# Convolution stage: two output weights loaded after the last way back, one tap ordered behind a low part, one tap moved ahead

## The chip, the cores and the metric

The kernel runs on one core of one Trainium2 chip. The time is that of one execution on the device in microseconds; a kernel's time is the median of several runs. The engines are named as in the profile: PE (TensorE, matrix products), DVE (VectorE), ACT (ScalarE), POOL (GpSimd), SP (SyncE, which issues most of the loads), and PEld for PE's weight loads.

## What is computed

Two layers of a trunk, each a token mixer followed by a SwiGLU network: first a convolution module, then sparse attention. SEQ is 512, D_MODEL 1024, float32 throughout. The change lies in the convolution module, the first 157 us:

```python
CONV_WIDTH = 31

def conformer_conv_module(h, w_in, b_in, w_dw, b_dw, ln_g, ln_b, w_out):
    a, g = jnp.split(h @ w_in + b_in, 2, axis=-1)
    u = a * jax.nn.sigmoid(g)
    u = lax.conv_general_dilated(
        u, w_dw[:, None, :].astype(u.dtype), window_strides=(1,),
        padding=[(CONV_WIDTH - 1, 0)], dimension_numbers=('NWC', 'WIO', 'NWC'),
        feature_group_count=D_MODEL) + b_dw
    uf = u.astype(jnp.float32)
    mu = jnp.mean(uf, axis=-1, keepdims=True)
    var = jnp.mean(jnp.square(uf - mu), axis=-1, keepdims=True)
    uf = (uf - mu) * lax.rsqrt(var + LN_EPS) * ln_g.astype(jnp.float32) + ln_b.astype(jnp.float32)
    u = jax.nn.silu(uf).astype(h.dtype)
    return u @ w_out
```

`h` is the normalised input. A projection gives `a` and `g`, the gated product `u` is convolved along time with 31 taps for each channel, normalised over the channels, and projected out. Then follow the network, the attention and a second network.

## The kernel before

**Chunks.** Channels lie on the 128 partitions, so the 1024 channels are 8 chunks of 128, and time (512) lies along the free axis.

**Weights.** Weights come in units of 128 x 1024 floats that are numbered in the order of use: 4 to 17 for chunks 1 to 7 of the input projection (two for each chunk, `a` and `g`), 18 to 21 for the first half of the output projection, 22 to 25 for its second half. A product in full precision is made of three: SP loads a raw tile `wr` (L216, three buffers), ACT copies its high part to `wh` (L226, two buffers), DVE subtracts to get the low part `wl` (L235, two buffers), and PE multiplies high by high (L286), high by low (L287) and low by high (L288). A weight's high part is requested one weight ahead of its use, its low part in the middle of the tile before.

**Who convolves.** After each projection the gate (`glu`, L488 to L498) makes the chunk's `u`, with DVE (L489, L492, L498) and ACT (L490). Chunk 0 is convolved on DVE, one `scalar_tensor_tensor` for each tap (L515). Chunks 2 and 3 share theirs: DVE does 22 and 18 taps, the other 9 and 13 are a product on ACT (L533, tile `tap`, four buffers) and an addition on POOL (L539), and L541 joins the halves. Chunk 1 is ACT and POOL alone. These taps of ACT and POOL stand in a list from which `some_taps` takes a few at a time: `TAPS_AT[i]` says how many ahead of and behind the `g` projection of chunk i. DVE's taps are issued with a high priority, so the scheduler fills them in between its other work.

**PE's chunks.** Chunks 4 to 7 are convolved on PE (L586, tile `cpe`). For that `u` is first rearranged by way of DRAM, eight phases of 64 time steps over 16 channels at a time: SP stores it (L560) and loads it back as `uf` (L561). The band matrices `bd` come by POOL's queue (L462), three buffers for four chunks. DVE evacuates the product (L590), ACT squares it (L592), SP stores the evacuated tile (L591) and loads it back in the order of channels (L568): the *way back*. Chunk 7 is done in four parts (`SPLIT`), and so are its evacuations and stores.

**Normalisation.** PE sums the convolved chunks and their squares over the channels (L637, `lnst`, for chunks 0 to 3; L649, `lng`, for chunks 4 to 7). ACT copies `lnst` (L656, `rows`), PE transposes it (L659, `lnrt`), DVE reduces both (L663 to `st`, L668 to `red`), and a chain of small steps on DVE, ACT and PE spreads mean and scale. Then for each chunk DVE subtracts and multiplies, ACT applies the activation twice (L798, `a` and `lny`), and DVE makes the low part (L784). The output projection begins with chunk 0 (L377, L378, L383) and goes on as the chunks are ready; each two chunks use one weight of 18 to 21.

**Order.** The order on each engine is fixed at build time by a scheduler. `after(a, b)` adds the condition that a stands behind b in that order, and no wait of its own. An engine runs its instructions in order, so whatever stands behind a waiting one waits too. Behind the last projection, L762 to L764 ask for weights 18 to 20 behind the load of chunk 7's `uf`, L766 keeps every later load of SP behind chunk 7's way back, and L768 and L769 ask for weight 18's parts.

Of the kernel before, what the change touches and what calls it, by code (L numbers as in the profile page):

```python
# [15 lines left out]
ALU = mybir.AluOpType  # L16
# [40 lines left out]
PE_CONV = (4, 5, 6, 7)  # L57
SHARED = {2: 9, 3: 13}
SHIFTED = (3,)
TAPS_AT = {2: (4, 3), 3: (4, 3), 4: (4, 3), 5: (4, 3), 6: (4, 3), 7: (4, 3)}  # L60
LN_ORDER = (0, 1, 2, 3)
BAND_BUFS = 3
SPLIT = {7: 2}
# [64 lines left out]
def trunk(ctx: ExitStack, tc: tile.TileContext, A, out):  # L128
    nc = tc.nc
# [8 lines left out]
    def nm(s):  # L138
        cnt[0] += 1
        return f"{s}_{cnt[0]}"  # L140
# [51 lines left out]
    raws, raw_dma, split, los = {}, {}, {}, set()  # L192
    pin = {}

    def after(a, b):

        if b is not None:
            tc.add_manual_dep(a.ins, b.ins.name, mybir.DependencyInfo(
                mybir.DependencyClass.NoSync, mybir.DependencyReason.DATA), reason="order")
        return a  # L200

    state = {"next": 0, "end": 18}
    hold = [False]

    def held(ins):
        return tc.keep_in_program_order(ins) if hold[0] else ins

    def parted(ins):
        return ins if hold[0] == "pe" else held(ins)

    def w_dma(i):
        if i in raws or i >= len(units):
            return
        ap, cols = units[i]
        t = wp.tile([P, 1024], F32, tag="wr", name=f"wr{i}")
        raw_dma[i] = parted(after(nc.sync.dma_start(t[:, :cols], ap), state.get("behind")))  # L216
        raws[i] = t
# [11 lines left out]
    def w_lo(i=None):  # L229
        i = state["next"] if i is None else i  # L230
        if i in los or i not in split:
            return
        cols = units[i][1]
        hi, lo = split[i]
        parted(after(nc.vector.tensor_tensor(lo[:, :cols], raws[i][:, :cols], hi[:, :cols], ALU.subtract), pin.get(ALU)))  # L235
        los.add(i)

    def next_w(ahead=True):

        i = state["next"]  # L240
        w_hi(i)
        w_lo(i)
        state["next"] += 1
        if ahead and i + 1 < state["end"]:
            w_hi(i + 1)
        for k in range(i, min(i + 4, state["end"])):
            w_dma(k)
        return split[i]
# [25 lines left out]
    def v(col, n=1):  # L274
        return vec[:, col:col + n]
# [74 lines left out]
    def norm_b(r, pool, tag):  # L350

        ps2 = pool.tile([P, T], F32, tag=tag, name=nm("rbc"))
        for t in range(4):
            held(nc.tensor.matmul(ps2[:, t * P:(t + 1) * P], r[:, t:t + 1].to_broadcast([P, P]), ident,
                                  start=True, stop=True))
        R = tp.tile([P, T], F32, tag="Rb", name=nm("Rb"), bufs=1)
        nc.scalar.activation(R, ps2, AF.Copy)
        return R
# [35 lines left out]
    def proj_tile(pool, tag, xh=None, xl=None, mid=None, fixed=False):  # L394
        xh, xl = xh or hh, xl or hl
        ps = pool.tile([P, T], F32, tag=tag, name=nm("pp"))
        wh, wl = next_w()
        for k in range(NK):
            c = slice(k * P, (k + 1) * P)
            if fixed:  # L400
                kept = tc.keep_in_program_order
                kept(nc.tensor.matmul(ps, wh[:, c], xh[k], start=k == 0, stop=False))
                kept(nc.tensor.matmul(ps, wh[:, c], xl[k], start=False, stop=False))
                kept(nc.tensor.matmul(ps, wl[:, c], xh[k], start=False, stop=k == NK - 1))
            else:
                mm3(ps, wh[:, c], wl[:, c], xh[k], xl[k], k == 0, k == NK - 1)
            if k == 3:
                w_lo()
                if mid:
                    mid()  # L410
        return ps
# [27 lines left out]
    def conv_module():  # L439
        acc = new_acc()  # L440
        with ExitStack() as cx:
# [25 lines left out]
            for k in range(NK):  # L467
                split_x(k, V_NM0)
                if k % 2 == 0:
                    wh, wl = next_w()  # L470
# [11 lines left out]
            last = {}  # L482
# [4 lines left out]
            def glu(i, pA, pG):  # L487
                gr = ct.tile([P, T], F32, tag="A", bufs=3, name=f"gr{i}")  # L488
                y = nc.vector.tensor_tensor(gr, pG, R, ALU.mult)  # L489
                last["glu_act"] = nc.scalar.activation(gr, gr, AF.Sigmoid, bias=v(V_BG + i))  # L490
                ar = pA
                after(nc.vector.tensor_tensor(ar, pA, R, ALU.mult), y)  # L492
                if i in PE_CONV:
                    dst = u[i][:, 32:].rearrange("p (r t) -> p t r", r=8)
                    ar, gr = (z.rearrange("p (t r) -> p t r", r=8) for z in (ar, gr))
                else:
                    dst = u[i][:, 32:]
                last["glu"] = nc.vector.scalar_tensor_tensor(dst, ar, v(V_BA + i), gr, ALU.add, ALU.mult)  # L498

            def wtap(i, j):  # L500
                return wdw[:, i * TAPS + j:i * TAPS + j + 1]

            def conv_dve(i):
                c = pc.tile([P, T], F32, tag="pc", name=f"cv{i}")
                if i in SHIFTED:
                    b = ct.tile([P, T], F32, tag="ptap", name=nm("bs"), bufs=1)
                    nc.scalar.activation(b, sh["s"], AF.Identity, scale=-1.0, bias=v(V_BDW + i))
                    z = nc.vector.scalar_tensor_tensor(c, u[i][:, 2:2 + T], wtap(i, 0), b, ALU.mult, ALU.add)
                else:
                    z = nc.vector.tensor_scalar(c, u[i][:, 2:2 + T], wtap(i, 0), v(V_BDW + i), ALU.mult, ALU.add)  # L510
                after(z, last.get("dve"))
                n = TAPS - SHARED.get(i, 0)
                for j in range(1, n):
                    dst = vch[i] if j == TAPS - 1 else c
                    last["dve"] = nc.vector.scalar_tensor_tensor(dst, u[i][:, 2 + j:2 + j + T], wtap(i, j), c,  # L515
                                                                 ALU.mult, ALU.add)
                if i in SHARED:
                    parts[i] = c
                vt[i] = vch[i]

            taps, parts = [], {}

            def conv_pool(i, j0=0):
                c = cp.tile([P, T], F32, tag="pacc", bufs=2, name=nm("pv"))
# [21 lines left out]
            def some_taps(n):  # L546
                for _ in range(n):
                    if taps:
                        taps.pop(0)()
# [152 lines left out]
            def after_glu(i):  # L702
                if i in PE_CONV:
                    ups[i] = conv_pe_load(i)
                else:
                    if i in POOL_CONV:
                        conv_pool(i)
                        return
                    if i not in SHIFTED:
                        conv_on_v(i)  # L710
# [7 lines left out]
            def at(i):  # L718
                for z in CONV_AT.get(i, ()):
                    if z == "s":  # L720
                        ln_shift(LN_ORDER[0])
                    elif z == "p":
                        some_taps(len(taps))
                    elif z[0] == "d":
                        conv_on_v(int(z[1:]))
                    elif z == "t":
                        ln_tok()
                    elif z == "w":
                        sh["w"] = pc.tile([P, T], F32, tag="pc", name="warm")
                    elif z[0] == "n":  # L730
                        sh[z] = ln_stat(LN_ORDER[int(z[1:])])
                    elif z[0] == "m":
                        ln_sum(int(z[1:]), sh["n" + z[1:]])
                    elif z[0] == "g":
                        ph_sum(int(z[1:]))
                    else:
                        c = int(z[1:])
                        conv_pe(PE_CONV.index(c), c, ups[c])

            for i in range(1, NK):  # L740
                pA = proj_tile(pm, "pm", mid=norm_1 if i == 1 else None, fixed=i == 1)

                def gated():
                    glu(i - 1, *pend)
                    after_glu(i - 1)

                def norm_2():
                    nonlocal R
                    R = norm_b(last["r"], pa, "pa")
                    gated()  # L750

                if i > 1:
                    gated()
                some_taps(TAPS_AT.get(i, (0, 0))[0])
                pG = proj_tile(pm, "pm", mid=norm_2 if i == 1 else None, fixed=i == 1)
                some_taps(TAPS_AT.get(i, (0, 0))[1])
                pend = (pA, pG)
                at(i)
            glu(NK - 1, *pend)
            after_glu(NK - 1)  # L760
            state["end"] = len(units)
            for k in range(18, 21):  # L762
                w_dma(k)
                after(raw_dma[k], last["load"])  # L764
            at(8)
            state["behind"] = last["back"]  # L766
            pin.update(last["evac"])
# [1462 lines left out]
```

## Time and profile before

| | us |
|---|---|
| time, median of 3 runs | 1188.76 |
| lowest and highest run | 1188.07 to 1189.54 |
| the profiled execution's own time | 1188.95 |
| its span (first to last instruction in the trace) | 1187.2 |
| PE busy | 1166.4 |
| DVE busy | 945.9 |
| ACT busy | 640.8 |
| POOL busy | 303.7 |

The profiled execution's time is 1.75 us longer than the span, which lies outside of the recorded instructions, and 0.19 longer than the median. The granted clock was 0.999 of full speed over the span, so no throttling has to be reckoned with.

In the rows below, a line of the totals gives busy time, share of the span and the count of instructions. A row of the waits says which engine and tile waited, for whom, and the sum, the count and the longest wait. A row of the timeline gives the start in us from the span's start, the stretch that the group occupies, engine, line, operation, tile written and tiles read, shapes, count, and in brackets the idle time before it and what ended it; "SPq" and "POOL DMA" are issues of transfers. A row of the windows gives, for a stretch of 2 us, its length and then for each of PE, PEld, DVE, ACT and POOL the busy time and the count, then the granted clock, the share of the DMA engines and the GB/s.

### The profile page before, as it was taken

The numbers are of one execution on the slowest core, as the hardware profiler recorded it, in microseconds if no ns is written. First come the engines' busy times: TensorE is split into PE (matmuls) and PEld (weight loads), VectorE is DVE, ScalarE is ACT, GpSimd is POOL, SyncE is SP. The second block draws the span as 40 slices with busy tenths as digits, with TensorE's granted clock in tenths as the row PEclk, the third lists the DMA queues.
The fourth block names the chain that finished last, engine by engine and source line by source line (L and its number), as shares of the span: only waits on it lengthen the run. The fifth ranks groups of instructions, "written<-read, shape, count | busy, mean of one in ns | idle before, by whom it ended". The sixth has DMA issues, their size and how long they took to land.

```text
span 1187.2 us, 20756 instructions
## 1 busy us (share of the span) xinstructions
PE 1166.4 (98%) x7653; PEld 993.2 (84%) x7653; DVE 945.9 (80%) x1872; ACT 640.8 (54%) x1199; POOL 303.7 (26%) x398
## 2 busy tenths in 40 slices
PE   9999999999999999999999999999999999999998
PEld 6778688799999889997778777668878999998998
DVE  6999797889999787972667778865597999986876
ACT  5665664455555445553444678773355555554543
POOL 2699001011111101210233566760000111110120
PEclk9999999999999999999999999999999999999999
DMA  8634627367777768663455101025324787775892
GB/s 301 264 109 132 181 91 228 107 170 188 186 189 186 182 188 196 125 188 97 128 153 157 46 19 36 10 71 143 107 94 137 185 186 186 184 192 143 230 187 98
DMA packets 80310, 178.13 MB, mean 150 GB/s; under 512 B 29264, under 2 KB 30928, under 8 KB 79184
## 3 DMA queue, kind: packets, MB, share of 16 engines
q1 hardware_dynamic: 56896, 105.78, 28.2%
q0 software_dynamic: 23312, 71.02, 26.8%
q8 instruction: 60, 0.98, 0.3%
q14 instruction: 42, 0.34, 0.1%
HBM read 161.93 MB, written 4.75 MB: 140 GB/s over the span
## 4 chain that ended last, share of the span: by engine, by line
PE 88%; DVE 6%; issue 2%; ACT 2%; DMA 1%; SPq 0%; POOL 0%; DVEq 0%; ACTq 0%; POOLq 0%
PE st L983 40%; PE pp L286 9%; PE pp L288 9%; PE pp L287 9%; PE O L1952 3%; PE T L1926 3%; PE S L1895 2%; PE cpe L586 2%; PE st L287 2%; PE st L286 2%; PE st L288 2%; PE S L1896 1%; DVE wl L235 1%; PE pv L1769 1%; PE pp L377 1%
## 5 line engine op out<-in xcount | busy, mean ns | idle before, releaser
L983 PE MATMUL st<-bo,sh 128*128 128x256 f32 (+1 forms) x952 | 245.6, 333 | 0.4 <-DVE t L1019 0.4
L226 ACT ACTIVATE wh<-wr 128x1024 fp32r<-128x1024 f32 (+3 forms) x146 | 151.2, 1035 | 166.7 <-issue 57.1
L235 DVE TENSOR_TENSOR wl<-wr,wh 128x1024 fp32r<-128x1024 f32 (+3 forms) x146 | 178.5, 1222 | 44.9 <-ACT wh L226 44.8
L983 PE MATMUL st<-bo,sl 128*128 128x256 f32 x680 | 191.7, 282 | 0.0
L983 PEld LDWEIGHTS st<-bo,sh 128*128 128x128 f32 x952 | 160.9, 189 | 20.2 <-DVE t L1019 1.2
L286 PE MATMUL pp<-hh,wh 128*128 128x512 f32 x400 | 158.6, 399 | 2.3 <-ACT wh L226 1.9
L288 PE MATMUL pp<-hh,wl 128*128 128x512 f32 x400 | 157.7, 397 | 2.2 <-DVE wl L235 2.2
L287 PE MATMUL pp<-hl,wh 128*128 128x512 f32 x400 | 157.5, 395 | 0.1
L983 PEld LDWEIGHTS st<-bo,sl 128*128 128x128 f32 x680 | 129.0, 190 | 0.0
L969 DVE TENSOR_TENSOR sl<-S,sh 128x512 fp32r<-128x512 f32 x136 | 90.6, 688 | 22.5 <-ACT sh L968 22.4
L983 PE MATMUL st<-bo,wh 128*128 128x256 f32 (+1 forms) x408 | 97.3, 316 | 0.0
L1913 POOL TENSOR_SCALAR Pm<-Pm,sm,gates 128x512 f32<-128x512 f32 (+3 forms) x128 | 81.2, 645 | 58.3 <-DVE sm L1909 38.0
L286 PEld LDWEIGHTS pp<-hh,wh 128*128 128x128 f32 x400 | 75.2, 188 | 22.9 <-ACT wh L226 3.7
L288 PEld LDWEIGHTS pp<-hh,wl 128*128 128x128 f32 x400 | 75.1, 188 | 21.0 <-DVE wl L235 3.4
L287 PEld LDWEIGHTS pp<-hl,wh 128*128 128x128 f32 x400 | 75.3, 188 | 17.4 <-DVE hl L321 0.5
L944 POOL DMA_DIRECT2D S<-fw_x x34 | 20.0, 588 | 267.3 <-DVE sl L969 265.9
L983 PE MATMUL st<-oz,soh 128*128 128x256 f32 x512 | 88.1, 277 | 0.0
L1899 ACT ACTIVATE Pm<-Pm,mx 128x512 f32<-128x512 f32 (+3 forms) x128 | 70.9, 555 | 31.6 <-DVE mx L1898 30.5
L1022 ACT ACTIVATE g<-g 128x512 f32<-128x512 f32 x34 | 21.5, 633 | 112.2 <-DVE g L1019 112.2
L983 PEld LDWEIGHTS st<-oz,soh 128*128 128x128 f32 x512 | 77.5, 188 | 0.5
L968 ACT ACTIVATE sh<-S 128x512 fp32r<-128x512 f32 x136 | 77.6, 619 | 0.0
L539 POOL TENSOR_TENSOR pv<-pv,tap 128x512 f32<-128x512 f32 x49 | 71.2, 1455 | 19.7 <-ACT tap L533 16.4
(314 smaller groups left out, 2735.5 us busy)
## 6 DMA issues: line engine op xcount, KB each, us to landing
S<-fw_x POOLq DMA_DIRECT2D x68, 512.0 KB, 6.0
wr<-fw_in SPq DMA_DIRECT2D x46, 512.0 KB
So<-fw_q POOLq DMA_DIRECT2D x38, 512.0 KB, 7.0
wr<-fw_q SPq DMA_DIRECT2D x24, 512.0 KB
bd<-bands POOLq DMA_DIRECT2D x8, 1280.0 KB, 13.9
r<-fw_x SPq DMA_DIRECT2D x34, 256.0 KB
wr<-cw_in SPq DMA_DIRECT2D x14, 512.0 KB
wr<-fw_p SPq DMA_DIRECT2D x12, 512.0 KB
```

Of the source, the lines that this page charges most:

```text
L226: state["wh"] = parted(after(nc.scalar.activation(hi[:, :cols], raws[i][:, :cols], AF.Copy), pin.get(AF)))
L235: parted(after(nc.vector.tensor_tensor(lo[:, :cols], raws[i][:, :cols], hi[:, :cols], ALU.subtract), pin.get(ALU)))
L286: held(nc.tensor.matmul(ps, wh, xh, start=first, stop=False))
L287: held(nc.tensor.matmul(ps, wh, xl, start=False, stop=False))
L288: held(nc.tensor.matmul(ps, wl, xh, start=False, stop=last))
L539: last["pool"] = after(nc.gpsimd.tensor_tensor(dst, c, z, ALU.add), last.get("pool"))
L968: pe(nc.scalar.activation(h_[:, c], z, AF.Copy))
L969: pe(nc.vector.tensor_tensor(l_[:, c], z, h_[:, c], ALU.subtract))
L983: nc.tensor.matmul(out, a[:, k], b, start=f, stop=z, skip_group_check=True))
L1899: kept(nc.scalar.activation(Pt, Pt, AF.Exp, bias=mx, scale=-1.0, accum_out=sm))
L1913: kept(nc.gpsimd.tensor_scalar(Pt, Pt, sm[:, k:k + 1], gates[:, t + k, br * 16 + h:br * 16 + h + 1], ALU.mult, ALU.mult))
L1926: pe(nc.tensor.transpose(pt[:, c:c + P], u["P"][:, o:o + P], ident))
```

## The change

It has three parts.

```diff
+LOW_AT = 9
-TAPS_AT = {2: (4, 3), 3: (4, 3), 4: (4, 3), 5: (4, 3), 6: (4, 3), 7: (4, 3)}
+TAPS_AT = {2: (4, 3), 3: (4, 3), 4: (4, 3), 5: (4, 3), 6: (4, 3), 7: (4, 4)}
...
-        parted(after(nc.vector.tensor_tensor(lo[:, :cols], raws[i][:, :cols], hi[:, :cols], ALU.subtract), pin.get(ALU)))
+        state["wl"] = parted(after(nc.vector.tensor_tensor(lo[:, :cols], raws[i][:, :cols], hi[:, :cols], ALU.subtract), pin.get(ALU)))
...
+                    dve_taps.append(last["dve"])
...
-            taps, parts = [], {}
+            taps, parts, dve_taps = [], {}, []
...
+                if i == 3:
+                    after(dve_taps[LOW_AT], state["wl"])
...
-            for k in range(18, 21):
-                w_dma(k)
-                after(raw_dma[k], last["load"])
+            w_dma(18)
+            after(raw_dma[18], last["load"])
```

First, in the third projection, a tap of chunk 0 on DVE is ordered behind the low part of weight 9. Second, one more of the taps of ACT and POOL is taken ahead of the gate of chunk 7, 4 in place of 3. Third, of weights 18 to 20 only 18 is loaded behind chunk 7's `uf`; 19 and 20 are asked for where 21 was, by the ordinary requests of the output projection, and so stand behind chunk 7's way back on SP.

The lines of the changed kernel are 1 to 5 higher than those of the one before (L515 becomes L516, L235 becomes L236, L590 becomes L592). The scheduler's order shows what the parts move.

DVE, where the high part of weight 9 has just been made (`pp` and `Rb` are the gate's inputs, `u2` its result, `cv0` chunk 0 under convolution), before:

```order
L492 TENSOR_TENSOR pp_37_429<-pp_37_429,Rb_36_378 128x512
L515 SCALAR_TENSOR_TENSOR cv0_385<-u0_141,wdw_102,cv0_385 128x512
L498 SCALAR_TENSOR_TENSOR u2_143<-pp_37_429,vec_74,gr2_547 128x512
L515 SCALAR_TENSOR_TENSOR cv0_385<-u0_141,wdw_102,cv0_385 128x512 x4
L235 TENSOR_TENSOR wl9_518<-wr9_433,wh9_517 128x1024
L515 SCALAR_TENSOR_TENSOR cv0_385<-u0_141,wdw_102,cv0_385 128x512 x3
L235 TENSOR_TENSOR wl10_590<-wr10_480,wh10_589 128x1024
```

And now:

```order
L493 TENSOR_TENSOR pp_37_429<-pp_37_429,Rb_36_378 128x512
L516 SCALAR_TENSOR_TENSOR cv0_385<-u0_141,wdw_102,cv0_385 128x512
L499 SCALAR_TENSOR_TENSOR u2_143<-pp_37_429,vec_74,gr2_547 128x512
L516 SCALAR_TENSOR_TENSOR cv0_385<-u0_141,wdw_102,cv0_385 128x512
L236 TENSOR_TENSOR wl9_518<-wr9_433,wh9_517 128x1024
L516 SCALAR_TENSOR_TENSOR cv0_385<-u0_141,wdw_102,cv0_385 128x512 x3
L236 TENSOR_TENSOR wl10_590<-wr10_480,wh10_589 128x1024
```

One tap instead of four stands ahead of the low part. Three taps are gone from this place, and from here on every tap of DVE stands three places later among the other work.

DVE behind the last projection, from the evacuation of chunk 5 (`uf5`) to the four of chunk 7 (`uf7`), before:

```order
L590 TENSOR_TENSOR uf5_877<-cpe5_1130,nb5_1128 128x8x64
L515 SCALAR_TENSOR_TENSOR cv3_726<-u3_144,wdw_102,cv3_726 128x512 x7
L590 TENSOR_TENSOR uf6_967<-cpe6_1219,nb6_1217 128x8x64
L541 TENSOR_TENSOR u3_144<-cv3_726,pv_67_747 128x512
L590 TENSOR_TENSOR uf7_1115<-cpe7_1356,nb7_1354 128x2x64
L590 TENSOR_TENSOR uf7_1115<-cpe7_1380,nb7_1354 128x2x64
L235 TENSOR_TENSOR wl18_1477<-wr18_1120,wh18_1476 128x1024
```

And now:

```order
L592 TENSOR_TENSOR uf5_877<-cpe5_1129,nb5_1127 128x8x64
L516 SCALAR_TENSOR_TENSOR cv3_726<-u3_144,wdw_102,cv3_726 128x512 x7
L592 TENSOR_TENSOR uf6_967<-cpe6_1218,nb6_1216 128x8x64
L516 SCALAR_TENSOR_TENSOR cv3_726<-u3_144,wdw_102,cv3_726 128x512 x3
L543 TENSOR_TENSOR u3_144<-cv3_726,pv_67_747 128x512
L592 TENSOR_TENSOR uf7_1118<-cpe7_1352,nb7_1350 128x2x64
L592 TENSOR_TENSOR uf7_1118<-cpe7_1376,nb7_1350 128x2x64
L236 TENSOR_TENSOR wl18_1473<-wr18_1123,wh18_1472 128x1024
```

The last three taps of chunk 3 now stand behind the evacuation of chunk 6, ahead of the join (L541, now L543) and of chunk 7's evacuations.

SP behind the last projection, the stores of chunks 4 to 7 (`swap<-uf`), the ways back (`u<-swap`) and the weights, before, from weight 18 on:

```order
L216 DMA wr18_1120<-cw_os 128x1024
L216 DMA wr19_1122<-cw_os 128x1024
L591 DMA swap_96_1020<-uf4_784 1024x1x64
L216 DMA wr20_1124<-cw_os 128x1024
L591 DMA swap_98_1127<-uf5_877 1024x1x64
L568 DMA u4_145<-swap_96_1020 128x8x64
...
L591 DMA swap_111_1353<-uf7_1115 128x2x64 x2
L568 DMA u7_148<-swap_111_1353 128x8x64
L216 DMA wr21_1533<-cw_os 128x1024
```

And now:

```order
L217 DMA wr18_1123<-cw_os 128x1024
L593 DMA swap_97_1023<-uf4_784 1024x1x64
L593 DMA swap_99_1126<-uf5_877 1024x1x64
L570 DMA u4_145<-swap_97_1023 128x8x64
...
L593 DMA swap_111_1349<-uf7_1118 128x2x64 x3
L570 DMA u7_148<-swap_111_1349 128x8x64
L217 DMA wr19_1526<-cw_os 128x1024
L217 DMA wr20_1531<-cw_os 128x1024
L217 DMA wr21_1533<-cw_os 128x1024
```

Weights 19 and 20 have moved behind the last load of chunk 7's way back, just ahead of 21. The ways back of chunks 5 and 6 stand one or two stores earlier than before; the other loads and stores keep their order.

On ACT and POOL the one tap moves ahead of the gate of chunk 7, and on POOL its addition ahead of the last bands' load, so that 11 additions instead of 10 stand ahead of it there. In the attention stage, some 500 us later, the order on DVE and ACT changes in one place: the compressed softmax (its `cl` and `sc`) stands ahead of four mask reductions (L1898). PE's order there is unchanged.

## The prediction

> **What bounds the kernel now.** I read the page first (share of each engine), then what PE waits for, then the chain of waits between 85 and 165 us, where all three edits lie, then the timelines of the engines there.
>
> ```profile
> PE 1166.4 (98%) x7653; PEld 993.2 (84%) x7653; DVE 945.9 (80%) x1872; ACT 640.8 (54%) x1199; POOL 303.7 (26%) x398
> PE cpe L586 <- issue: 3.1, 2, 2.3
> PE pp L288 <- DVE wl L235: 2.2, 2, 1.7
> ```
>
> PE is busy for 98% of the span, so only PE's waits and the few stretches where PE hangs on a chain of other engines can give time. The last two rows are PE's longest waits: 3.1 us in the phase products of the convolution (`cpe`), and 2.2 us for low parts of weights, 1.7 of it in one piece. The change touches both neighbourhoods. All that follows 135 us is PE work that the change leaves as it is, so what counts is when the first output product starts, at 134.57.
>
> **The tap behind the low part.** DVE, then PE, around weight 9:
>
> ```profile
> 44.44 1.05 ACT L226 ACTIVATE wh<-wr 128x1024 fp32r<-128x1024 f32 x1
> 45.61 3.12 DVE L515 SCALAR_TENSOR_TENSOR cv<-u,wdw,cv 128x512 f32<-128x512 f32 x4
> 48.64 2.08 DVE L235 TENSOR_TENSOR wl<-wr,wh 128x1024 fp32r<-128x1024 f32 x1
> 48.70 0.39 PE L287 MATMUL pp<-hl,wh 128*128 128x512 f32 x1
> 50.77 0.51 PE L288 MATMUL pp<-hh,wl 128*128 128x512 f32 x1 [1.68 <-DVE wl L235]
> ```
>
> The high part is ready at 44.44 + 1.05 = 45.5, but four taps stand ahead of the low part on DVE, and PE waits until 50.77. With one tap ahead instead of four (pitch 3.03/4 = 0.76) the low part starts at 46.4 and ends at 47.6 to 48.5: durations of this form in the trace are 1.22 (at 124.49, below) and 2.08 here. PE wants it at 48.70 + 0.23 = 48.9. The wait goes: **-1.7 us** on PE (bounds -1.3 and -1.8). Between 50.8 and the end of the projections at 102.4 PE has no other wait above half a microsecond, and DVE is three taps (2.3) ahead while PE is 1.7 ahead, so nothing on DVE is late. POOL does not move with them; that is the second rival.
>
> **The same three taps, later.** The order on DVE shows that the debt is paid after the last projection, between the evacuations of chunks 6 and 7:
>
> ```profile
> 102.44 0.69 DVE L489 TENSOR_TENSOR gr<-pp,Rb 128x512 f32<-128x512 f32 x1 [0.55 <-PE pp L288]
> 115.86 5.50 DVE L515 SCALAR_TENSOR_TENSOR cv<-u,wdw,cv 128x512 f32<-128x512 f32 x7
> 121.26 0.68 DVE L590 TENSOR_TENSOR uf<-cpe,nb 128x512 f32<-128x512 f32 x1
> 122.46 0.28 DVE L590 TENSOR_TENSOR uf<-cpe,nb 128x128 f32<-128x128 f32 x1
> 124.28 0.29 DVE L590 TENSOR_TENSOR uf<-cpe,nb 128x128 f32<-128x128 f32 x1 [1.53 <-PE cpe L586]
> 124.49 1.22 DVE L235 TENSOR_TENSOR wl<-wr,wh 128x1024 fp32r<-128x1024 f32 x1
> 125.62 0.28 DVE L590 TENSOR_TENSOR uf<-cpe,nb 128x128 f32<-128x128 f32 x1
> 126.68 0.29 DVE L590 TENSOR_TENSOR uf<-cpe,nb 128x128 f32<-128x128 f32 x1 [0.78 <-PE cpe L586]
> 120.59 2.54 PE L586 MATMUL cpe<-uf,bd 128*64 128x64 f32 x79
> 123.97 2.23 PE L586 MATMUL cpe<-uf,bd 128*64 128x64 f32 x66 [0.83 <-issue]
> ```
>
> From 102.44 to 122.46, the first of chunk 7's four evacuations, DVE works without a gap: 20.0 us. It now starts at 102.44 - 1.7 = 100.7 and has three taps more, 3 x 5.40/7 = 2.3, so that evacuation starts at 100.7 + 20.0 + 2.3 = 123.0, 0.6 *later* than before. The next fixed distance is by way of ACT, which squares and then makes weight 18's high part: from the first evacuation to the low part, 124.49 - 122.46 = 2.0. So the low part at 125.1, the third evacuation 1.13 behind it, at 126.2, the fourth 0.2 on, at 126.4 (before: 126.68). What vanishes is DVE's waiting for PE, 1.53 + 0.78. PE holds nothing up there: the rows at 120.59 and 123.97 hold 145 of its products in 4.8 us, and even with both of its stalls (2.3 and 0.8 of the 3.1 under "issue" above) it has the last quarter done by about 125. For the same reason I give **nothing** for those stalls, whether the lighter DMA load shortens them or not.
>
> Behind the fourth evacuation:
>
> ```profile
> 126.58 0.62 PE L637 MATMUL lnst<-u,onesb 128*32 128x512 f32 x1
> 128.24 0.27 PE L649 MATMUL lng<-nb,ph 128*32 128x128 f32 x1
> 128.85 0.69 DVE L668 TENSOR_REDUCE red<-lng 128x64 f32<-128x512 f32 x1 [1.87 <-PE lng L649]
> 129.46 0.17 DVE L663 TENSOR_REDUCE st<-lnrt 128x8 f32<-128x16 f32 x1
> 127.01 0.31 ACT L592 ACTIVATE nb<-uf 128x128 f32<-128x128 f32 x1 [0.77 <-DVE uf L590]
> 127.73 0.60 ACT L656 ACTIVATE rows<-lnst 128x512 f32<-128x512 f32 x1 [0.41 <-PE lnst L637]
> 128.45 0.66 PE L659 MATMUL lnrt<-cc,rows 128*128 128x128 f32 x4
> 134.57 0.50 PE L377 MATMUL pp<-a,wh 128*128 128x512 f32 x1 [0.55 <-ACT a L798]
> ```
>
> Before, PE had 24 statistics products left when chunk 7's products ended (126.58 to 128.5), and `red` waited for them. Now nearly all of them run before the fourth evacuation. Left behind it: the square (0.33 + 0.31, ending 127.05), one pair of products and the hand-over (128.85 - 128.24 = 0.6), `red` at 127.7, ending 128.3. Beside it ACT's `rows` at 127.05 (before 127.73), the transposes 0.7 later until 128.4, so L663 at about 128.4 instead of 129.46: **-1.1**, and the rest to the first output product is the same chain: 133.5.
>
> **The two weights.** Weight 18 stays early. 19 and 20 now leave SP behind chunk 7's way back.
>
> ```profile
> 130.80 0.88 SPq L591 DMA_DIRECT2D swap<-uf  x2
> 134.56 0.36 SPq L568 DMA_DIRECT2D u<-swap  x1
> 134.97 0.57 SPq L216 DMA_DIRECT2D wr<-cw_os  x1
> 135.13 1.04 ACT L226 ACTIVATE wh<-wr 128x1024 fp32r<-128x1024 f32 x1
> 136.08 0.80 ACT L798 ACTIVATE a<-u,vec 128x512 fp32r<-128x512 f32 x1
> 137.47 0.40 PE L377 MATMUL pp<-a,wh 128*128 128x512 f32 x1
> 134.00:136.00 2.00, 1.45 (x7) 1.21 (x7) 1.69 (x4) 2.00 (x3) 0.00 (x0) 1.00 0.11 26
> 136.00:138.00 2.00, 2.00 (x10) 1.59 (x10) 2.00 (x3) 1.58 (x3) 0.00 (x0) 1.00 1.06 338
> 138.00:140.00 2.00, 2.00 (x10) 1.63 (x9) 1.97 (x4) 1.52 (x2) 0.00 (x0) 1.00 0.61 182
> ```
>
> This adds a wait: weight 19's high part stands on ACT ahead of chunk 1's activation (136.08), which PE needs at its second step (137.47). The last store can go at 126.7. The last two stores are issued from 130.80 to 131.68, the second near 131.2; the load that waits for it (`u<-swap`, the way back) goes at 134.56, 3.3 later. So the way back leaves by about 130.0 and weight 19 0.4 behind it, at 130.4. The last column of the windows is GB/s: by 138.0 some 0.73 MB had gone since the way back left, of the 0.79 that it and weight 21 are, so that weight was there 3.4 us after its issue, 138.3. Weight 19 by the same: 133.8. ACT wants it at 135.13 - 1.1 = 134.0, and the activation behind it has 137.47 - 136.88 = 0.6 to spare. **Cost 0**, bounds 0 and +0.5 (a landing 1.1 later than that, which the spare no longer covers in full: 0.2 + 0.6 of slack leaves 0.3, rounded up). Weight 20 is wanted 5 us later and is hidden; 21 leaves earlier than before.
>
> The Trainium skill (DMA: Bandwidth & Descriptors, "Queues, rings and completion order") says that a semaphore's increment lands only after all earlier writes of that DMA engine, whatever the queue. By it weight 19 cannot be reported before the way back has landed, as I reckoned; without it the weight could be there over a microsecond sooner, and the third rival would be smaller. No row here separates the two.
>
> **The tap by the last column, and small moves.**
>
> ```profile
> 103.16 0.72 ACT L490 ACTIVATE gr<-gr,vec 128x512 f32<-128x512 f32 x1 [3.41 <-DVE gr L489]
> 104.64 4.29 POOL L539 TENSOR_TENSOR pv<-pv,tap 128x512 f32<-128x512 f32 x3 [0.29 <-ACT tap L533]
> 108.86 1.10 POOL L462 DMA_DIRECT2D bd<-bands  x2
> DMA to landing us min/median/max: 6.2/8.1/10.0
> 666.31 1.10 PE L1634 MATMUL psc<-kcb,qraw 128*128 128x64 f32 x8 [0.88 <-ACT t L1931]
> ```
>
> The tap fills 0.6 of 3.4 idle us of ACT. It also puts one POOL addition (1.4) ahead of the last bands' load and saves a 0.3 wait: the load leaves 1.1 later and its second half is there by 109.4 + 10.0 + 1.1 = 120.5, about when chunk 6's evacuation (now near 120) frees the product's bank: 0. In the attention stage (648 to 660 us) the compressed softmax moves ahead of four mask reductions on DVE, with PE's order unchanged: 0, bounds -0.9 and +0.9, PE's nearest wait being 0.88.
>
> **Sum.** -1.1 + 0 + 0 = -1.1 on the profiled execution's 1188.95 (span 1187.2): 1187.85. The median shown is 0.19 lower: 1187.6. Unknown terms reach from -1.7 (the whole PE wait kept) to +0.5, and 0.9 each way for the attention stage.
>
> **The rivals.**
>
> *Nothing (16%).* The DVE tail takes all back. For: it is already 0.6 later at chunk 7's first evacuation, and a further 0.7 would do. The nearest cause: POOL is not sped up, a ScalarE tap waits for a POOL addition to free its buffer, and a high part stands behind such taps; one addition is 1.35. About -0.2: 1188.6.
>
> *More (10%).* Unlike what I reckon, DVE's debt is paid in its own idle time (0.55 at 102, and its waits for PE), and PE's "issue" stalls shrink too, so the tail is PE's: 1.7 and one to two of the 3.1: -2.8, 1186.0. Against: the order rows show the three taps behind 102.
>
> *Slower (9%): weight 19 is late.* Mechanism: its load leaves last of all of SP's work, and ACT blocks in front of chunk 1's activation. It decides from a landing at about 134.6. If it came as late as weight 21 did (138.3), ACT would lose 138.3 - 135.1 - 0.6 = 2.6 against before: 1191.4. For: no slack to speak of beyond 0.6. Against: the three transfers that held SP up to 119 are two fewer.
>
> **How the numbers follow.** The forecast (within 0.7 of -1.1) has 65%. Faster by over 0.2% means below 1186.4, slower above 1191.1; 0.2% is about what a measurement of this kernel can tell from no change. "More" gives 8 points of faster, the forecast's lower edge with the attention bound 4: 12%. "Slower" gives 6. The rest, 82%, is within 0.2%. The range, 1186.0 to 1189.8, takes in "more" at its value and the upper bounds, and leaves out about 15%.
>
> **What would show it.** PE's wait for `wl` of 1.68 gone near 49 us; the last projection's end near 100.7; chunk 7's first evacuation near 123.0 and its fourth near 126.4; the first output product at 133.5; ACT's high part of weight 19 without a long wait. The forecast is wrong if that high part starts over 0.6 behind the first activation pair, or if PE waits anew between 51 and 100.

## The result and the profile after

The changed kernel is slower: 1196.20 us (median of 6 runs, 1194.79 to 1198.05) against 1188.74 (6 runs), a ratio of 1.0065 with a 95% interval from 1.0052 to 1.0078. The time lies outside of the range that was given, on the side of the third rival.

The profiled execution took 1194.79, with a span of 1193.0. Totals of the page, and PE's longest wait, after:

```profile
PE 1172.0 (98%) x7653; PEld 996.3 (84%) x7653; DVE 947.6 (79%) x1872; ACT 641.8 (54%) x1199; POOL 304.0 (25%) x398
PE pp L378 <- ACT a L801: 4.3, 2, 3.8
```

PE is counted as busy 5.6 us longer for the same 7653 products, and its idle time is about what it was (1187.2 - 1166.4 = 20.8, now 21.0): the totals alone would hide that a new wait, 3.8 us for an activation of the output projection, has come in the place of old ones. So the stage has to be read, in order of time. DVE and PE around weight 9, from the timeline of after:

```profile
46.52 1.72 DVE L236 TENSOR_TENSOR wl<-wr,wh 128x1024 fp32r<-128x1024 f32 x1
48.48 0.40 PE L289 MATMUL pp<-hh,wl 128*128 128x512 f32 x1
100.57 14.12 PE L588 MATMUL cpe<-uf,bd 128*64 128x64 f32 x470
```

The low part is there by 48.2, PE uses it at 48.48 without a wait, and the last projection ends 1.76 earlier (102.33 before, 100.57 now). The first part of the change does what it says. DVE's tail, after, with one row of before (the one at 104.30) for comparison:

```profile
100.68 0.69 DVE L490 TENSOR_TENSOR gr<-pp,Rb 128x512 f32<-128x512 f32 x1
105.78 1.66 DVE L509 SCALAR_TENSOR_TENSOR cv<-u,wdw,bs 128x512 f32<-128x512 f32 x1
121.02 2.33 DVE L516 SCALAR_TENSOR_TENSOR cv<-u,wdw,cv 128x512 f32<-128x512 f32 x3
124.06 0.48 DVE L592 TENSOR_TENSOR uf<-cpe,nb 128x128 f32<-128x128 f32 x2
127.19 0.48 DVE L592 TENSOR_TENSOR uf<-cpe,nb 128x128 f32<-128x128 f32 x2
...
104.30 0.75 DVE L508 SCALAR_TENSOR_TENSOR cv<-u,wdw,bs 128x512 f32<-128x512 f32 x1
```

From the gate of chunk 7 to its first evacuation it is 23.4 us (20.0 before): 2.3 for the three taps, and 0.9 because the first tap of chunk 3 took 1.66 instead of 0.75. Then SP, after, with one row of before (the one at 129.95):

```profile
123.35 3.60 SPq L593 DMA_DIRECT2D swap<-uf  x2
128.91 0.36 SPq L570 DMA_DIRECT2D u<-swap  x1
129.37 1.62 SPq L593 DMA_DIRECT2D swap<-uf  x3
134.09 0.36 SPq L570 DMA_DIRECT2D u<-swap  x1
134.56 1.47 SPq L217 DMA_DIRECT2D wr<-cw_os  x3
...
129.95 0.36 SPq L568 DMA_DIRECT2D u<-swap  x1
```

The two stores from 123.35 on are chunk 6's and chunk 7's first. Behind them stands chunk 6's way back, at 128.91, and only behind that chunk 7's other three stores, though the tile of the last was ready at 127.7. Chunk 7's way back goes at 134.09, weights 19 to 21 behind it. Then ACT and PE, after, and the windows (last four columns: POOL, granted clock, share of the DMA engines, GB/s); the last PE row is from before:

```profile
134.10 0.80 ACT L801 ACTIVATE lny<-u,vec 128x512 f32<-128x512 f32 x1
139.26 1.06 ACT L227 ACTIVATE wh<-wr 128x1024 fp32r<-128x1024 f32 x1 [4.36 <-DMA wr<-cw_os]
134.25 0.50 PE L378 MATMUL pp<-a,wh 128*128 128x512 f32 x1 [0.55 <-ACT a L801]
136.21 1.10 PE L384 MATMUL pp<-a,wh 128*128 128x512 f32 x4
141.07 0.50 PE L378 MATMUL pp<-a,wh 128*128 128x512 f32 x1 [3.77 <-ACT a L801]
143.01 0.63 PE L378 MATMUL pp<-a,wh 128*128 128x512 f32 x1
145.52 0.40 PE L378 MATMUL pp<-a,wh 128*128 128x512 f32 x1
138.00:140.00 2.00, 0.00 (x0) 0.00 (x0) 0.00 (x0) 0.74 (x1) 0.00 (x0) 1.00 0.92 338
142.00:144.00 2.00, 2.00 (x7) 1.52 (x6) 1.97 (x4) 1.52 (x2) 0.00 (x0) 0.51 0.68 219
144.00:146.00 2.00, 2.00 (x8) 1.57 (x7) 1.72 (x3) 0.23 (x1) 0.00 (x0) 0.64 0.11 43
146.00:148.00 2.00, 2.00 (x10) 1.64 (x9) 1.14 (x1) 2.00 (x3) 0.00 (x0) 1.00 0.00 0
...
140.28 0.39 PE L377 MATMUL pp<-a,wh 128*128 128x512 f32 x1
```

The sum can be read off. The first output product starts at 134.25 (134.57 before): -0.32. The second step waits, since ACT has weight 19's high part ahead of its activation and the weight lands at 139.2: it starts at 141.07 (137.47), now +3.60. Then its twelve products take 145.52 - 141.07 = 4.45 (140.28 - 137.47 = 2.81): 1.64 more, +5.24. One product takes 0.63 there instead of 0.40, and the granted clock is a half from about 142.0 to 145.4. The rest of the program adds 0.6 in pieces of both signs under a microsecond (0.5 of it in the attention stage), which makes the 5.8 between the spans. The medians differ by 7.5: the profiled execution was the fastest of the six. Two of the others list a mean clock of 0.994 instead of its 0.997.

### The profile page after: what moved, and what is told of

It is laid out like the page before. It is cut to its first block, busy times and chain, and to the rows that moved or that the text cites. A ratio compares the mean times of both kernels' runs of the same rounds, so it can differ in the third digit from the quotient of the medians.

```text
span 1193.0 us, 20754 instructions
## 1 busy us (share of the span) xinstructions
PE 1172.0 (98%) x7653; PEld 996.3 (84%) x7653; DVE 947.6 (79%) x1872; ACT 641.8 (54%) x1199; POOL 304.0 (25%) x398
## 4 chain that ended last, share of the span: by engine, by line
PE 83%; DVE 10%; issue 3%; ACT 2%; DMA 1%; POOL 0%; SPq 0%; DVEq 0%; POOLq 0%; ACTq 0%
PE st L986 39%; PE pp L287 8%; PE pp L289 8%; PE pp L288 8%; PE O L1955 3%; PE T L1929 3%; DVE cv L516 3%; PE S L1898 2%; DVE wl L236 2%; PE st L288 2%; PE st L287 2%; PE st L289 2%; PE S L1899 1%; DVE Pm L1901 1%; PE pp L384 1%
## 5 line engine op out<-in xcount | busy, mean ns | idle before, releaser
L236 DVE TENSOR_TENSOR wl<-wr,wh 128x1024 fp32r<-128x1024 f32 (+3 forms) x146 | 179.3, 1228 | 52.1 <-ACT wh L227 52.0
L541 POOL TENSOR_TENSOR pv<-pv,tap 128x512 f32<-128x512 f32 x49 | 71.5, 1460 | 18.9 <-ACT tap L535 15.4
```

What stands on the lines that cost most here:

```text
L236: state["wl"] = parted(after(nc.vector.tensor_tensor(lo[:, :cols], raws[i][:, :cols], hi[:, :cols], ALU.subtract), pin.get(ALU)))
L541: last["pool"] = after(nc.gpsimd.tensor_tensor(dst, c, z, ALU.add), last.get("pool"))
```

## The experiments

Two theories at the start. **W**: the late weight is the whole loss, first as a wait, then as a lower clock. **T**: the taps' debt in DVE's tail pushes the stores and makes the weight late. Each kernel ran beside the kernel before on the same chip (medians of before: 1187.95 for the first four, 1188.08 for the next, 1188.66 for the last).

**1. The weights alone, weights_only.**

```diff
-            for k in range(18, 21):
-                w_dma(k)
-                after(raw_dma[k], last["load"])
+            w_dma(18)
+            after(raw_dma[18], last["load"])
```

> The kernel before, with weights 19 and 20 loaded behind chunk 7's way back and neither of the other two parts. Theory W (the loss is weight 19's late load, and then PE's clock): the way back left SP at 134.56 before and leaves about there again, weight 19 lands at 138.5 to 139.5, PE waits 3 to 4 us ahead of its second step and then runs 1 to 2 us longer at half the granted clock: +4.5 to +6.5 us. Rival T (the tail: the three taps push chunk 7's stores, and the weight is late only for that): without the taps the way back leaves by 131 and the loss is 0 to +2 us.

Measured: 1193.43, ratio 1.0043 (1.0027 to 1.0058), +5.5 us. SP, ACT and two windows of weights_only:

```profile
134.02 0.36 SPq L568 DMA_DIRECT2D u<-swap  x1
138.69 1.06 ACT L226 ACTIVATE wh<-wr 128x1024 fp32r<-128x1024 f32 x1 [4.82 <-DMA wr<-cw_os]
142.00:144.00 2.00, 2.00 (x6) 1.60 (x5) 1.97 (x4) 1.16 (x2) 0.00 (x0) 0.50 0.81 262
144.00:146.00 2.00, 2.00 (x6) 1.53 (x5) 1.13 (x2) 0.00 (x0) 0.00 (x0) 0.50 0.00 0
```

With no tap moved the way back goes at the same time, 134.02, the weight is as late and the clock falls as well. T falls as the cause of the large loss.

**2. The tap order alone, low_only**: the changed kernel with the weights and `TAPS_AT` of before.

> The kernel before, with only the tap of chunk 0 ordered behind weight 9's low part. Theory W: the 1.7 us wait of PE for that low part goes, the convolution's tail on DVE gives most of it back, the first output product starts 0.3 to 1.0 earlier: -0.3 to -1.0 us. Rival T: the longer tail costs by itself: +1 to +3 us.

Measured: 1189.62, 1.0012 (1.0004 to 1.0021), +1.7 us. W missed here, and T's number came. But the profile doesn't show it in the tail: the first output product starts at 133.74, 0.8 earlier than before. It shows it 500 us later (waits of PE from 645 to 675 us, low_only):

```profile
PE S L1899 <- DVE mx L1902: 1.5, 2, 0.8
```

Before has no such row there. That is the attention stage, where the same edit had moved the compressed softmax ahead of four mask reductions. It became theory **A**, runs 9 and 10.

**3. Both tap parts without the weights, no_weights** (the early loads of 18 to 20 put back).

> The changed kernel with weights 18 to 20 early as before (both tap parts stay). Theory W: the half-clock stretch and the wait at the second output step are gone, -0.3 to -1.0 us against before, that is 7 to 8.5 less than the changed kernel. Rival T: +1 to +3 against before.

Measured: 1188.47, 1.0006 (0.9996 to 1.0015). Between W's and T's numbers, and by the two ratios 7.0 less than the changed kernel: the loss goes with the weights. From low_only this kernel differs by the tap in `TAPS_AT` alone: 1.15 less here, with overlapping intervals.

**4. Weight 19 early, 20 late, one_late** (`range(18, 20)` in the loop).

> The changed kernel with weights 18 and 19 early, and only 20 behind the way back. Theory W: only weight 19 is wanted before the way back has landed; weight 20 lands at about 139.5 and is wanted at 140, so no wait of PE over 0.5: -1.0 to +0.3 us against before. Rival T: as no_weights, +1 to +3.

Measured: 1189.24, 1.0012 (1.0002 to 1.0022). No wait for an activation over 0.5 is left among PE's longest, so weight 20 may be late and only 19 may not. That the time is still 1.3 above before is again T's number and not W's.

**5. Chunk 6's way back behind chunk 7's stores, backs_last.**

```diff
-                if len(ups) == len(PE_CONV):
+                if len(ups) == len(PE_CONV) and i != 6:
                     send_backs()
...
-                    nc.sync.dma_start(phase[:, gs], ce[:, gs])
+                    last["st"] = nc.sync.dma_start(phase[:, gs], ce[:, gs])
...
-                    last["back"] = after(nc.sync.dma_start(*backs.pop(0)), last["load"])
+                    last["back"] = after(after(nc.sync.dma_start(*backs.pop(0)), last["load"]), last["st"])
```

> The changed kernel with chunk 6's way back ordered behind the last store of chunk 7 on SP. Theory W, with the queue as its cause (three of chunk 7's stores stand behind chunk 6's way back, which waits at the head of SP until 128.9 for its own store): the last store leaves near 128 instead of 130.9, chunk 7's way back at 131 to 132.5 instead of 134.1, weight 19 lands at 135 to 137, PE waits under 2.5 us and keeps its clock: 4 to 6 us less than the changed kernel, 1190 to 1192. Rival (the stores are slow in themselves, under the load on the DMA engines): way back at 133.5 or later, weight 19 beyond 138.5, 1195 to 1197.

Measured: 1189.91, 1.0014 (1.0005 to 1.0023), by the two ratios 6.1 less than the changed kernel. SP, ACT and PE of backs_last:

```profile
123.42 5.24 SPq L593 DMA_DIRECT2D swap<-uf  x5
129.07 1.73 SPq L570 DMA_DIRECT2D u<-swap  x2
130.91 2.80 SPq L217 DMA_DIRECT2D wr<-cw_os  x3
135.80 1.06 ACT L227 ACTIVATE wh<-wr 128x1024 fp32r<-128x1024 f32 x1 [1.41 <-DMA wr<-cw_os]
137.62 0.50 PE L378 MATMUL pp<-a,wh 128*128 128x512 f32 x1 [0.80 <-ACT a L801]
```

The five stores are out by 128.7, the weight leaves at 130.91 instead of 134.56 and is there 3.5 earlier, and PE waits 0.8. So the place of chunk 6's way back on SP had held weight 19 up; it was shown by moving that one transfer. Of the 3.65 that weight 19 leaves earlier, 2.3 is the last store's earlier issue (128.7 instead of 131.0). The other 1.3 is a shorter time from there to chunk 7's way back, and whether that comes of less traffic was not tested.

**6. Work for PE in the gap, warm_fill**: 13 products on zeros behind the first output step.

```diff
+                if low_last and k == 0:
+                    spare = pool.tile([P, T], F32, tag=tag, name="spare")
+                    for _ in range(13):
+                        kept(nc.tensor.matmul(spare.rearrange("p (a b) -> p a b", a=4), zb,
+                                              zb[:, None, :].to_broadcast([P, 4, P]), start=True, stop=True))
```

> The changed kernel with 13 products on zeros (the form of L312) on PE behind the first output step, in the place where PE was empty for 3.8 us. Theory (the granted clock falls to half because PE is empty): weight 19 and PE's second step come when they did, near 141.1, but the clock stays at 1.0 and the second step takes 2.9 instead of 4.5 us: 1.4 to 1.8 less than the changed kernel. Rival (the slow products come of the weights and activations that land and are made just then): the second step takes 4.5 again, no gain.

Measured: 1195.02, 1.0054 (1.0039 to 1.0068); by the two ratios 1.3 less than the changed kernel, with overlapping intervals. The second step took 3.0 at a granted clock of 1.0, but in the profiled execution weight 19 happened to come at 137.3, two us earlier, so that PE would not have been empty for long in any case. Inconclusive; runs 11 and 12 repeat it with a longer gap.

**7. Weight 19 between the ways back, mid**, without the tap parts, and **8. the same in the changed kernel, mid_tap**:

```diff
-                    nc.sync.dma_start(phase[:, gs], ce[:, gs])
+                    st = nc.sync.dma_start(phase[:, gs], ce[:, gs])
+                    if i == 7 and g0 == 0:
+                        w_dma(19)
+                        after(raw_dma[19], last["back"])
+                    elif i == 7:
+                        after(st, raw_dma[19])
```

> The kernel before with weight 18 early, weight 19 on SP between chunk 6's way back and chunk 7's last three stores, weight 20 and 21 behind chunk 7's way back; no tap moved. Theory W: weight 19 leaves at 129 to 130 onto idle DMA engines, lands by 133.5, no wait for it, and the first output product keeps the 1.3 us that weights_only had: -0.8 to -1.6 us against before. Rival (with the fewer early loads the tail is no faster, that lead was chance): -0.3 to +0.5.

> The changed kernel with weight 19 in the place that mid gives it. Theory W: no wait and no half clock; the first output product at 134.0 to 134.3 as in the changed kernel, so -0.3 to -0.6 against before, and 0.5 to 1 slower than mid, since the taps' debt in DVE's tail stays. Rival T: the tail costs by itself, +1 to +3 against before.

Measured: mid 1187.73, 0.9991 (0.9983 to 1.0000); mid_tap 1189.64, 1.0011 (1.0001 to 1.0020). No wait for weight 19 in either: ACT takes its high part at 135.54 and 135.05, right behind `lny`. mid's lead is that of its rival, not of W: its first output product came at 134.99, so the early 133.22 of weights_only did not come again. The two profiles are not quite alike there: in mid the granted clock is a half from 118.6 to 122.0, among the products of the convolution, in weights_only it is not. mid_tap is 1.6 above before, T's number for the third time, and 1.9 behind mid.

**9. low_only with the attention order of before, low_attn**, and **10. the same on mid_tap, mid_tap_attn**. `M` are the mask reductions, `g` the gates' three steps, `c` those of the compressed softmax's sums, `sms` the reciprocals:

```diff
+            line = [M[0], seq["valid"], g0, M[1], c0, M[2], g1, sms[0], M[3], c1, g2, c2, M[4], sms[1], c3, M[5],
+                    seq["weighed"], M[6]]
+            for y, z in zip(line, line[1:]):
+                after(z, y)
```

> low_only with the order of the attention stage on DVE held as the kernel before has it (the compressed softmax among the first mask reductions; one low part and one reciprocal stay a place off). Theory A (what low_only lost against its shorter convolution is that reorder, which makes PE wait for mask reductions near 655 us): no wait of PE for mx there, 1.0 to 2.0 us less than low_only, -0.8 to +0.2 against before. Rival T (the longer tail on DVE costs by itself): +1.2 to +2.0 against before, as low_only.

> mid_tap with the attention stage's order held in the same way. Theory A: 0.4 to 1.5 less than mid_tap, -0.5 to +0.6 against before, near mid. Rival T: as mid_tap, +1 to +2.

Measured: low_attn 1187.42, 0.9990 (0.9981 to 0.9999), where low_only had 1.0012 (1.0004 to 1.0021); mid_tap_attn 1188.77, 1.0001 (0.9992 to 1.0010). PE's waits from 645 to 675 us in low_attn, all of them:

```profile
PE psc L1639 <- ACT t L1950: 0.9, 1, 0.9
PE T L1945 <- DVE pcl L1696: 0.2, 1, 0.2
```

The wait for `mx` is gone, and with it the loss: by the two ratios low_attn is some 2.6 us faster than low_only, and its interval lies below 1. These two profiles alone don't prove A, since low_attn has the half clock there (645.1 to 648.5) and low_only has not, and at half clock PE waits only 0.3 for `mx` with the new order too (no_weights, one_late, mid_tap). But at full clock low_only, warm_fill, gap_long and gap_fill, with the new order, all wait 1.5 for `mx`, and mid_tap_attn, with the old one, doesn't. So A holds, though the stage accounts for 0.5 to 1.8 us (below) and not for all of the 2.6. T falls for low_only too: from chunk 7's gate to its first evacuation the tail is 23.4 us in both. On mid_tap the step is in the same direction, inside of overlapping intervals. low_attn is the only kernel of the study whose interval lies wholly below that of before.

**11 and 12. A longer gap, empty and filled, gap_long and gap_fill**: in both, `w_dma(20)` and `w_dma(21)` stand ahead of `proj_start`, so 19 leaves last; gap_fill also has warm_fill's edit with 26 products.

> The changed kernel with weights 20 and 21 asked for ahead of 19, so that 19 leaves SP last, 1.0 to 1.5 us later than in the changed kernel. PE waits 5 to 7 us ahead of its second step. Clock theory (PE empty for over some 3.4 us is given half the clock for some 3.4 us): the granted clock is 0.5 in the 2 us windows behind it, the second step takes 4.2 to 5 us instead of 2.9. Rival (traffic, not emptiness): as in the changed kernel at most, and the same with the fill.

> gap_long with 26 products on zeros (the form of L312) behind PE's first output step, some 6 us of work in the wait. Clock theory: the granted clock stays 1.0, the second step takes 2.9 us, 1.4 to 2 us less than gap_long. Rival (traffic): the second step takes over 4 us again, no gain.

Measured: gap_long 1194.53 (1.0053, 1.0038 to 1.0068), gap_fill 1201.42 (1.0110, 1.0094 to 1.0125). PE and a window of gap_long:

```profile
144.31 0.79 PE L378 MATMUL pp<-a,wh 128*128 128x512 f32 x1 [5.08 <-ACT a L801]
149.17 0.39 PE L378 MATMUL pp<-a,wh 128*128 128x512 f32 x1
144.00:146.00 2.00, 1.70 (x4) 1.24 (x5) 2.00 (x4) 2.00 (x4) 0.00 (x0) 0.50 0.06 18
```

And of gap_fill:

```profile
136.26 5.79 PE L392 MATMUL spare<-zb 128*128 128x512 bf16 x26
141.69 0.58 PE L378 MATMUL pp<-a,wh 128*128 128x512 f32 x1
144.69 0.40 PE L378 MATMUL pp<-a,wh 128*128 128x512 f32 x1
144.00:146.00 2.00, 2.00 (x10) 1.63 (x9) 2.00 (x3) 1.52 (x3) 0.00 (x0) 1.00 0.51 154
```

On the clock the reading is plain: after 5.1 us with nothing to do the next step of PE takes 149.17 - 144.31 = 4.86 at a granted clock of 0.5; with the fill a step takes 144.69 - 141.69 = 3.0 at 1.0, though more is moved meanwhile (154 GB/s against 18 in the windows shown). In gap_long the clock was a half from 141.7 on, with nothing at all moved from 142 to 144. So traffic is not what slowed PE. On the time the expectation failed: the scheduler put the wait of gap_long behind the second step, while the fill stands behind the first, so the fill delayed a step that had nothing to wait for, and later weights with it: PE waited 1.5 and 2.0 us for a high and a low part near 152, and the clock was a half from 155.4 to 158.9.

## Why the prediction was wrong

- **"The wait goes: -1.7 us on PE"**: right; the last projection ended 1.76 earlier.
- **"Three taps more, 3 x 5.40/7 = 2.3"**: mis-sized. The tail grew by 3.4, and the first output product gained 0.3 instead of 1.1. 0.9 of it is one instruction, the first tap of chunk 3, 1.66 instead of 0.75; all eleven profiles with the tap order show 1.54 to 1.68 for it, the three without 0.75 or 0.76. Why was not found. Beside the scatter of this product from execution to execution (133.22 and 134.99 in two kernels with the same taps) the miss is small.
- **"The last store can go at 126.7 ... so the way back leaves by about 130.0"**: this is the step that failed. I let the store go when its tile was ready (127.7 in fact), and forgot what stands ahead of it on SP. Chunk 6's way back waits at the head of the queue for its own store, until 128.91, and three of chunk 7's stores wait behind it. The rows of before showed it, a way back at 129.95 and the last two stores behind it at 130.80, and I used only the distance behind them. The way back went at 134.09, where it had gone before (134.56). Run 5 moved that one transfer and got most of the loss back.
- **"Cost 0, bounds 0 and +0.5" for weight 19**: with the way back 4.1 later the weight came at 139.2, 4.6 behind its slack. The rival "slower" had this mechanism and its place right, at 9%. Its price, 2.6, lacked two things: the clock, and 0.9 of the landing, which was later than the 138.3 that I took over from weight 21. 20 and 21 were under way with 19, which may be the reason; no run has 19 there alone.
- **The clock** is in no term of the prediction. PE had no work from 137.3 to 141.07, and the granted clock then was a half for about 3.4 us: +1.64. The mean of 0.999 over the span of the kernel before was read as no throttling, but a mean over 1187 us hides such a piece, and that kernel has one in the attention stage. PE's wait there ends at 645.19, and the clock (third column from the right) is a half from 645.4 to 648.8; before:

```profile
PE bc L1378 <- DVE qraw L1380: 1.9, 1, 1.9
644.00:646.00 2.00, 0.81 (x3) 0.72 (x4) 2.00 (x4) 0.45 (x1) 1.03 (x2) 0.84 0.87 293
646.00:648.00 2.00, 2.00 (x11) 2.00 (x10) 2.00 (x5) 0.00 (x0) 0.00 (x0) 0.50 0.70 205
```

The Trainium skill (TensorE: Matmul & The Clock Gate, "HAM oscillation — how this bites in real kernels") gives as a rule that PE should have no gap above some 3.4 us. This case agrees for the long ones: gaps of 3.8, 4.2 (weights_only) and 5.1 us brought a half clock, one of 0.8 (backs_last) did not, and products on zeros in the gap kept it at 1.0 (gap_fill). But shorter gaps brought it too: the 1.9 above does in eight of the 14 profiles and not in the other six. So a gap under 3.4 us is not safe here; the last section has what sets the two groups apart.

- **"0, bounds -0.9 and +0.9" for the attention stage**: the sign was left open, and it was a cost. PE waited 0.3 there for `mx` in the changed kernel and 1.5 in low_only. From the product behind the wait for `qraw` (645.19 in before) to the first of `psc` (666.31) it is 21.1 us before and 21.6 after. All nine profiles with the new order take 21.6, at half clock or at full; those with the old order take 21.1 where the half clock falls there (before, weights_only, low_attn) and 19.9 where it doesn't (mid, mid_tap_attn). So the new order costs 0.5 or 1.8 us, as the clock happens to be. PE's order being unchanged did not protect it: DVE's had changed ahead of what PE waits for.
- **The tap by the last column** was not run on the kernel before; added to low_only it gave no_weights, which lost nothing by it. In the profiles that have it PE waits 1.0 to 1.7 for chunk 7's bands in several executions (`cpe <- DMA bd<-bands`), ahead of the evacuations that DVE does later anyway. Its own price stays open.

## What to carry to other kernels

A transfer issued from an in-order queue leaves when everything ahead of it on that queue has left, waits included; a load moved behind a chain is to be timed from the rows of the whole queue, not from the moment at which its own input is ready. A wait on the busiest engine is to be priced twice: the wait, and the clock that can fall behind it, here even behind a wait of 1.9 us. And an edit that a scheduler sees may reorder a stage far away: compare the order of the whole program, and price what moved there with the waits of its own neighbours.

## What the runs showed of the hardware beside that

By the granted clock of their windows, the half clock lasted 6.8 us in gap_long (from about 141.7 to 148.5, the gap being 5.1) and 6.8 in weights_only (gap 4.2), twice the 3.4 of the changed kernel (gap 3.8). In gap_long it began while PE was still empty, in the changed kernel 1.0 behind PE's first product. So the stretch did not follow the length of the gap; in all profiles it came in pieces of 3.4.

The pieces lie on a grid. By windows of 0.1 us the clock falls at 142.04 and 650.62 in the changed kernel, 149.0 times 3.413 us apart; in gap_long at 141.69 and 674.17, 156.0 times. Whole multiples come out in all of the seven profiles with two such falls ahead of the program's end. With the grid laid through each trace by its own falls (in low_only by the one behind its last instruction), the 1.9 us gap of the attention stage lies whole inside one cell in the eight profiles where the clock then fell. In the six others a cell's edge cuts it: in mid at 644.27, into 0.7 and 1.2. The reading that fits is that the clock is set anew every 3.41 us by how long PE was idle in the cell just past. It is inferred from these traces, no run moved a gap across an edge by intent, and the limit is not sharp: a cell with 1.8 us idle was followed by a half clock in mid_tap and not in mid_tap_attn, and near 672 in gap_long and warm_fill one with 1.2 was. It may be a part of why one kernel's times scatter, since the same wait would be charged or not as the grid falls.
